# A hybrid attention and DeltaNet block on one core: query and key projections with two terms in one instruction, inverses by alternate columns, transfers and output banks on other queues and pools

## The chip, the core and the metric

The kernel runs on one core of a Trainium2 chip. The core has a matrix engine (PE, whose weight loads the profile lists as PEld), a vector engine (DVE), a scalar engine (ACT), a general engine (POOL) and a queue engine (SP) that here only issues transfers. ACT and POOL can issue transfers too. Each engine works through its own list of instructions in order and waits for the others by semaphores. The metric is the device time of the program in microseconds (us), the median of several runs.

## What is computed

One decoder layer over 256 positions of 1024 channels, all in float32. The input `x` is normalised to `h`; one projection gives twelve parts. Two branches follow: causal softmax attention of 8 heads (suffix `a`), and a gated delta rule of 8 heads in chunks of 64 (suffix `b`). Both are gated, projected, merged and projected again.

```python
h = rmsnorm(x, pre_norm_w)
proj = jnp.einsum('bsd,de->bse', h, w_in)              # 1024 -> 10256
(q_a, k_a, v_a, z_a, q_b, k_b, v_b, z_b, beta_logit, decay_logit, gate_a, gate_b) = jnp.split(proj, IN_OFFSETS, axis=-1)
o_a = moba_attention(partial_rope(heads(q_a), pos), partial_rope(heads(k_a), pos), heads(v_a))
y_a = (o_a * silu(z_a)) @ w_branch_a
q_b, k_b, v_b = split(silu(causal_dwconv(concat(q_b, k_b, v_b), conv_w)))
o_b = gated_deltanet(q_b, k_b, v_b, g, beta)           # solves (I + M) sol = rhs, M strictly lower
y_b = (rmsnorm(o_b, gdn_norm_w) * silu(z_b)) @ w_branch_b
merged = sigmoid(gate_a) * y_a + sigmoid(gate_b) * y_b
return x + rmsnorm(merged @ w_out, post_norm_w)
```

## The kernel before

**Numbers.** A plain float32 product takes several passes of PE. The large projections are therefore made of three products in the one-pass type `float32r`: each operand is split into a high part and the rest, and `hi*Hh + hi*Hl + lo*Hh` are summed in one bank of PSUM. `hi` and `lo` belong to a weight tile, `Hh` and `Hl` to the transposed normalised input (`Xh`, `Xl` to the input without its row factor).

**Slots.** The weights come in 104 slots, in a fixed order (`add`, `pair`, `piece`): v of `a` (slots 0 to 7); then four groups of six slots with two each of k of `b`, q of `b`, q of `a` (8 to 31); four groups of two v of `b` and two k of `a` (32 to 47); the z's (48 to 63), the gates (64 to 79), the branch projections `wa`, `wb` (80 to 95) and the output projection `wo` (96 to 103). For each slot SP loads `raw` (`load`, five buffers in turn), ACT copies it to `hi`, and DVE makes `lo` from both (`prep`). A load is issued when the `lo` of five slots before is made. `projT` makes 128 channels by 256 positions with 24 matmuls of 256 columns; `projN` makes 12 matmuls of 512 columns.

**The planner.** The work around the projections is written as Python generators: `conv` (three steps `acc` on DVE), `unit` (per head k·k and q·k, tile `kk`, then `Mall` and `AV`), `factors`, `inverses`, `vnat`, `head` (the delta rule, tile `dl`), `ybtask`, `ropetask`, `att`, `merge`. While PE's list is written, `tick()` lets each generator go on whose input is ready by a table of costs (`cost_v`, `cost_a`, `dma`, `at`). So each engine's order is fixed when the program is built. DVE and ACT run what the planner put in their lists, in that order, even when a later instruction could already start.

**Banks.** PSUM has three banks for projections (`psP`, taken by `palloc`, given back by `pfree`) and five for the other work (`psM`, taken by `take` or `mbank`, given back by `give`).

**Inverses.** After `factors` has scaled `Mall`, `inverses` (L772) inverts the 64 diagonal 32x32 blocks by substitution, all at once on 128 partitions. Four ACT transfers write the blocks to DRAM (`dN`), two read them back transposed (`Nt`); 31 steps j follow, two DVE instructions each on `m` columns by `31 - j` rows (tile `NtTt`). Each partition has 16 columns of its block, the even partitions 0 to 15 and the odd ones 16 to 31, so `m = min(j + 1, 16)` columns are not zero at step j. Then ACT writes the result to DRAM (`dT`) and reads it back in four transfers (`DT`), for which `head` waits.

**Decays.** `betadecay` (L590) loads 16 rows of decays (`Grow`), subtracts in four DVE instructions of 512 elements in a row, and ACT takes absolute value and exponential in eight.

**Rope.** `ropetask` turns q and k of `a` in six DVE instructions (tile `rt`) after transfers on POOL, and writes them back through DRAM on POOL (`dq2`, then `qa`, `ka`), for which `att` waits.

**The end.** `merge` transposes the merged rows into a `psM` bank (tile `mT`), from which ACT and DVE make `mH`, `mL`; slots `wo` use four more `psM` banks (`po`).

Of the kernel before, what the change touches and what calls it, by code (L numbers as in the profile page):

```python
# [9 lines left out]
F32 = mybir.dt.float32  # L10
# [27 lines left out]
def tile_moba_gdn_block(  # L38
# [108 lines left out]
        q.dma_start(dst, src)  # L147

    cst = ctx.enter_context(tc.tile_pool(name="cst", bufs=1))
    big = ctx.enter_context(tc.tile_pool(name="big", bufs=11))  # L150
    dp = ctx.enter_context(tc.tile_pool(name="dp", bufs=16))
    wp = ctx.enter_context(tc.tile_pool(name="wp", bufs=4))
    tmp = ctx.enter_context(tc.tile_pool(name="tmp", bufs=2))
# [5 lines left out]
    def bigt(name, dt=F32):  # L159
        return big.tile([P, 2048], dt, tag="big", name=name)  # L160
# [245 lines left out]
        return ps  # L406


    def projN(i, pss, lh, ll, kk):
        wh, wl = wts.pop(i)  # L410
        order = [(j, t, m) for j in range(2) for t in range(NT) for m in range(3)]
        if kk == 3 or i == 4:
            order.sort(key=lambda e: e[1])
        if i < 3:
            order.sort(key=lambda e: (e[2] == 2, e[1]))
        for n, (j, t, m) in enumerate(order):
            k = 2 * kk + j
# [65 lines left out]
    gdnw = parT[:, 96:97]  # L483
    Xh = bigt("Xh", F32R).rearrange("p (k s) -> p k s", k=KT)
    Xl = bigt("Xl", F32R).rearrange("p (k s) -> p k s", k=KT)
    Hh = bigt("Hh", F32R).rearrange("p (k s) -> p k s", k=KT)
    Hl = bigt("Hl", F32R).rearrange("p (k s) -> p k s", k=KT)
    xh, xl = (lambda k: Xh[:, k, :]), (lambda k: Xl[:, k, :])
    hh, hl = (lambda k: Hh[:, k, :]), (lambda k: Hl[:, k, :])

# [29 lines left out]
    for _ in xrows(0):  # L520
        pass
    at(clk["T"])
    warmup(8)
    at(0.0)
    prepnow(0, True)

# [63 lines left out]
    def betadecay():  # L590
# [69 lines left out]
        for q in range(4):  # L660
            us = slice(4 * q, 4 * q + 4)
            V.tensor_tensor(Grow[:, us, :], Grow[:, us, :], sm[:, GN, us].unsqueeze(2).to_broadcast([P, 4, P]),
                            op=OP.subtract)
        yield
        act(sm[:, EGL, :], sm[:, EGL, :], AF.Exp)
        for q in range(4):
            us = slice(4 * q, 4 * q + 4)
# [104 lines left out]
    def inverses():  # L772
        yield from need("fac0", "fac1")

        dN = dr.tile([4, 16, 32, 32], F32, name="dN")
        NT_ = bigt("NtTt")
        Nt = NT_[:, 0:1024].rearrange("p (i j) -> p i j", i=32)
        Tt = NT_[:, 1024:1536].rearrange("p (c i) -> p c i", c=16)
        op = NT_[:, 1536:2048].rearrange("p (c i) -> p c i", c=16)
        DT[0] = bigt("DT").rearrange("p (u s) -> p u s", u=16)  # L780
        yield
        for b in range(4):
            dma(nc.scalar, dN[b].rearrange("u i j -> i u j"), Mall[32 * b:32 * b + 32, :, 32 * b:32 * b + 32])
        t0 = cur[0]
        dma(nc.gpsimd, Tt.rearrange("p c i -> p (c i)"), c_rope[:, 512:1024])
        G.memset(DT[0], 0.0)
        at(t0)
        yield
        for hf in range(2):
            dma(nc.scalar, Nt[hf:P:2].rearrange("p i j -> p (i j)"), dN.rearrange("b u i j -> (b u) (i j)"))  # L790
        yield
        for b in range(4):
            t0 = cur[0]
            G.memset(Mall[32 * b:32 * b + 32, :, 32 * b:32 * b + 32], 0.0)
            at(t0)
        for j in range(31):
            n = 31 - j

            m = min(j + 1, 16)
            V.tensor_tensor(op[:, :m, :n], Tt[:, :m, j:j + 1].to_broadcast([P, m, n]),  # L800
                            Nt[:, j + 1:32, j].unsqueeze(1).to_broadcast([P, m, n]), op=OP.mult)
            V.tensor_tensor(Tt[:, :m, j + 1:32], Tt[:, :m, j + 1:32], op[:, :m, :n], op=OP.subtract)
            if j % 2 == 1:

                at(cur[0] - 2.0)
                yield
        dT = dr.tile([4, 16, 32, 32], F32, name="dT")
        yield
        dma(nc.scalar, dT.rearrange("b u c i -> (b u c i)").rearrange("(p n) -> p n", p=P), Tt.rearrange("p c i -> p (c i)"))
        yield  # L810
        for b in range(4):
            dma(nc.scalar, DT[0][32 * b:32 * b + 32, :, 32 * b:32 * b + 32], dT[b].rearrange("u c i -> c u i"))
        at(cur[0] + 5.0)
        done("dt")

    def vnat(h, v2):
# [282 lines left out]
    for i, (kind, n, src, c0) in enumerate(slots):  # L1099
# [20 lines left out]
        elif kind in ("qa", "ka"):  # L1120
            dst = qa if kind == "qa" else ka
            if n == 0:
                dst[0] = bigt(kind).rearrange("p (k s) -> p k s", k=KT)
            ps = projT(i, hh, hl, f"p{kind}{n}")
            act(dst[0][:, n, :], ps, AF.Copy)
            pfree(pids[0] - 1)
            done(f"{kind}{n}")
        elif kind == "va":
# [30 lines left out]
        elif kind in ("wa", "wb"):  # L1159
# [6 lines left out]
            if kk == 0:  # L1166
                grp[kind] = [palloc(f"p{kind}{c}{t}") for t in range(NT)]
                if kind == "wa" and c == 0:
                    mH = bigt("mH", F32R).rearrange("p (k s) -> p k s", k=KT)
                    mL = bigt("mL", F32R).rearrange("p (k s) -> p k s", k=KT)  # L1170
                    xr = bigt("xr").rearrange("p (t d) -> p t d", t=NT)
                    pwt = bigt("pwt")[:, 0:D]
                    ob = bigt("ob").rearrange("p (t d) -> p t d", t=NT)
# [18 lines left out]
        elif kind == "wo":  # L1192
# [3 lines left out]
                grp["wo"] = {}  # L1196
                act(warm[:, 129:130], tw, AF.Sqrt)
            if kk == 0:
                grp["wo"][c] = [mbank(f"po{t}{c}") for t in range(NT)]
            for t in range(NT):  # L1200
                drain(f"mg{kk // 2}{t}")
                at(max(cur[0], flags[f"mg{kk // 2}{t}"]))
# [25 lines left out]
def _constants():  # L1228
# [9 lines left out]
    tt = np.zeros((P, 16, 32), np.float32)  # L1238
    for p in range(P):
        for c in range(16):  # L1240
            tt[p, c, 16 * (p % 2) + c] = 1.0
    rope[:, 512:1024] = tt.reshape(P, 512)
    return {"c_sq": sq, "c_rope": rope}

# [24 lines left out]
```

## Time and profile before

| | us |
|---|---|
| median of 3 runs | 381.87 |
| lowest and highest run | 380.86, 381.88 |
| the profiled execution, its own time | 381.31 |
| its span in the trace | 379.6 |
| PE busy | 365.5 (96%) |
| DVE busy | 279.5 (74%) |
| ACT busy | 202.5 (53%) |
| POOL busy | 29.9 (8%) |

The span begins at the first instruction and ends at the last; 1.7 us of the profiled execution's time lie outside it. A matmul's row covers its way through the engine, and the next one begins before it has ended. So the cost of one in a row of them is the distance from start to start, and a busy share of 96% does not say that PE loses only 4%. A wait for several things is put down to the one that came last.

### The profile page before, as it was taken

Reading aid. Unit: us, or ns where it says so; the run is one execution under the profiler, and the core shown is the slowest. Engines: PE = TensorE matmul, PEld = TensorE weight load, DVE = VectorE, ACT = ScalarE, POOL = GpSimd, SP = SyncE. Lnnn points to the kernel's source line nnn. Section 1 sums busy time; section 2 is a strip of 40 time slices with the busy share of each in tenths; the row PEclk is TensorE's granted clock in tenths of the full one; section 3 lists DMA queues with packets and bytes.
Section 4 is the critical chain, followed back from the end, with each engine's and each line's share of the span. In section 5 each row is a group of like instructions: output and inputs, shape, how many; then the busy total and the mean of one; then the engine's idle time right before and its main releaser. Section 6 shows DMA issues by size and latency. Waiting matters only on the chain.

```text
span 379.6 us, 6307 instructions
## 1 busy us (share of the span) xinstructions
PE 365.5 (96%) x2300; PEld 326.2 (86%) x2300; DVE 279.5 (74%) x639; ACT 202.5 (53%) x405; POOL 29.9 (8%) x53
## 2 busy tenths in 40 slices
PE   8999999999999999989979999999999999999992
PEld 8777999999999999978868799989988888888681
DVE  3987895989987875999995364775898756666544
ACT  3758579455465546645433575456466753344431
POOL 2300000230200321011021000000100000000000
PEclk9999999999999999999999999999999999999998
DMA  7995954865767497469459943234634356656002
GB/s 232 354 255 141 244 145 108 221 168 130 205 167 182 135 237 226 129 180 265 144 179 287 260 142 108 59 108 112 212 107 139 103 165 208 181 172 202 14 0 111
DMA packets 70193, 63.92 MB, mean 168 GB/s; under 512 B 7793, under 2 KB 52194, under 8 KB 70162
## 3 DMA queue, kind: packets, MB, share of 16 engines
q1 hardware_dynamic: 61584, 56.50, 51.6%
q0 software_dynamic: 1680, 4.40, 3.9%
q10 hardware_dynamic: 6898, 2.62, 2.9%
q8 instruction: 18, 0.29, 0.3%
q14 instruction: 13, 0.11, 0.1%
HBM read 60.88 MB, written 2.63 MB: 167 GB/s over the span
## 4 chain that ended last, share of the span: by engine, by line
PE 72%; DVE 14%; DMA 5%; ACT 4%; issue 2%; ACTq 0%; DVEq 0%; POOL 0%; POOLq 0%
PE dl L129 7%; PE pva L129 6%; PE pgb L129 6%; PE pwa L129 6%; PE pga L129 6%; PE pwb L129 6%; PE po L129 6%; DVE lo L117 5%; PE pqb L129 5%; PE pqa L129 5%; DVE NtTt L117 5%; PE pkb L129 4%; PE pvb L129 3%; PE s L129 3%; DMA raw<-in_w_in_dram 3%
## 5 line engine op out<-in xcount | busy, mean ns | idle before, releaser
L117 DVE TENSOR_TENSOR lo<-raw,hi 128x1024 fp32r<-128x1024 f32 (+1 forms) x105 | 126.9, 1216 | 34.8 <-ACT hi L117 33.7
L117 ACT ACTIVATE hi<-raw 128x1024 fp32r<-128x1024 f32 x101 | 106.4, 1055 | 60.0 <-PE pza L129 13.3
L117 DVE TENSOR_TENSOR NtTt<-NtTt 128x112 f32<-128x112 f32 (+27 forms) x62 | 23.7, 382 | 3.0 <-DMA NtTt<-dN 1.3
L129 PE MATMUL pwa<-hi,ya 128*128 128x512 f32 x64 | 20.8, 399 | 0.0
L129 PE MATMUL pwb<-hi,yb 128*128 128x512 f32 x64 | 19.7, 389 | 0.0
L129 PE MATMUL pka<-Hh,hi 128*128 128x256 f32 x64 | 18.3, 287 | 0.7 <-DVE accv L117 0.7
L129 PE MATMUL pvb<-Hh,hi 128*128 128x256 f32 x64 | 18.9, 295 | 0.0
L129 PE MATMUL pkb<-Hh,hi 128*128 128x256 f32 x64 | 18.8, 293 | 0.0
L129 PE MATMUL pkb<-Hl,hi 128*128 128x256 f32 x64 | 18.2, 285 | 0.5 <-DVE Hl L117 0.5
L129 PE MATMUL pqb<-Hh,hi 128*128 128x256 f32 x64 | 18.6, 291 | 0.0
L129 PE MATMUL pqa<-Hh,hi 128*128 128x256 f32 x64 | 18.6, 290 | 0.0
L129 PE MATMUL pqb<-Hh,lo 128*128 128x256 f32 x64 | 18.2, 284 | 0.2 <-DVE lo L117 0.2
L129 PE MATMUL pqa<-Hh,lo 128*128 128x256 f32 x64 | 18.1, 283 | 0.0
L129 PE MATMUL pkb<-Hh,lo 128*128 128x256 f32 x64 | 18.1, 283 | 0.0
L129 PE MATMUL pqa<-Hl,hi 128*128 128x256 f32 x64 | 18.1, 283 | 0.0
L129 PE MATMUL pqb<-Hl,hi 128*128 128x256 f32 x64 | 18.1, 283 | 0.0
L129 PE MATMUL pka<-Hl,hi 128*128 128x256 f32 x64 | 18.1, 283 | 0.0
L129 PE MATMUL pka<-Hh,lo 128*128 128x256 f32 x64 | 18.1, 283 | 0.0
L129 PE MATMUL pvb<-Hh,lo 128*128 128x256 f32 x64 | 18.1, 283 | 0.0
L129 PE MATMUL pvb<-Hl,hi 128*128 128x256 f32 x64 | 18.1, 283 | 0.0
L117 DVE SCALAR_TENSOR_TENSOR acck<-pkb,parT,acck 128x255 f32<-128x255 f32 (+2 forms) x24 | 11.6, 481 | 7.9 <-ACT acck L117 7.3
L129 PE MATMUL pga<-hi,Hh 128*128 128x512 f32 x32 | 14.5, 453 | 0.3 <-ACT za L117 0.3
(383 smaller groups left out, 1041.5 us busy)
## 6 DMA issues: line engine op xcount, KB each, us to landing
raw<-in_w_in_dram SPq DMA_DIRECT2D x79, 512.0 KB, 4.4
raw<-in_w_branch_a_dram SPq DMA_DIRECT2D x8, 512.0 KB, 4.1
raw<-in_w_branch_b_dram SPq DMA_DIRECT2D x8, 512.0 KB, 4.1
raw<-in_w_out_dram SPq DMA_DIRECT2D x8, 512.0 KB, 4.3
x<-in_x_dram SPq DMA_DIRECT2D x4, 256.0 KB, 6.2
Grow<-dg ACTq DMA_DIRECT2D x2, 512.0 KB, 6.3
xr<-in_x_dram POOLq DMA_DIRECT2D x2, 512.0 KB, 3.9
out_dram<-ob SPq DMA_DIRECT2D x2, 320.0 KB, 2.2
```

The costliest lines, as they stand in the source:

```text
L117: LOG(self.e, c, fn(out, *a, **k))
L129: LOG("T", 0, nc.tensor.matmul(out, l, r, **k))
```

## The change

- `projH` takes the place of `projT` for q and k of `a` (16 slots). `Hh` and `Hl` now lie in one tile `H2`, so that `hi*Hh` and `hi*Hl` are one matmul of 512 columns into the two halves of a bank; `lo*Hh` stays one of 256 columns. ACT copies the second half, DVE adds the first one to it, and the bank is given back only then. 128 matmuls fewer are issued: 2088 before, 1956 after, with four warm-up matmuls that are dropped too.
- The warm-up after the first transposes is 4 matmuls, not 8.
- `betadecay` goes back to the planner after each of its four subtractions.
- In `inverses` the columns alternate between a pair of partitions, so that `m = j // 2 + 1`. The sum over the 31 steps of columns by rows is 2856, not 4776. `dN`, `Nt` and `DT` are issued by POOL and SP in turn, `DT` in eight pieces, not four. `dT` stays on ACT. The planner reckons `DT` to be there 16 us after `dT`, where it took 5 us after the last issue.
- `mH` and `mL` lie where `Hh` and `Hl` were, and the pool of large tiles has 9 buffers, not 11.
- The two `po` banks of the second half of the output come from `psP`, not from `psM`.

```diff
+    def projH(i, name):
+        hi, lo = wts.pop(i)
+        ps = palloc(name)
+        for k in range(KT):
+            for m in ((0, 1) if k == 0 else (1, 0)):
+                if m == 0:
+                    T.matmul(ps, hi[:, k, :], H2[:, :, k, :], start=(k == 0), stop=(k == KT - 1))
+                else:
+                    T.matmul(ps[:, 0:S], lo[:, k, :], Hh[:, k, :], start=False, stop=False)
+            if k < KT - 1:
+                tick()
+        return ps
...
+    H2 = cst.tile([P, 2, KT, S], F32R, name="H2")
+    Hh, Hl = H2[:, 0], H2[:, 1]
...
-    warmup(8)
+    warmup(4)
...
-        yield
+            yield 1.4
...
-            dma(nc.scalar, dN[b].rearrange("u i j -> i u j"), Mall[32 * b:32 * b + 32, :, 32 * b:32 * b + 32])
+            dma((nc.gpsimd, nc.sync)[b % 2], dN[b].rearrange("u i j -> i u j"), Mall[32 * b:32 * b + 32, :, 32 * b:32 * b + 32])
...
-            dma(nc.scalar, Nt[hf:P:2].rearrange("p i j -> p (i j)"), dN.rearrange("b u i j -> (b u) (i j)"))
+            dma((nc.gpsimd, nc.sync)[hf], Nt[hf:P:2].rearrange("p i j -> p (i j)"), dN.rearrange("b u i j -> (b u) (i j)"))
...
-            m = min(j + 1, 16)
+            m = j // 2 + 1
...
         for b in range(4):
-            dma(nc.scalar, DT[0][32 * b:32 * b + 32, :, 32 * b:32 * b + 32], dT[b].rearrange("u c i -> c u i"))
-        at(cur[0] + 5.0)
+            for e in range(2):
+                dma((nc.gpsimd, nc.sync)[e], DT[0][32 * b + e:32 * b + 32:2, :, 32 * b:32 * b + 32],
+                    dT[b, :, e].rearrange("u c i -> c u i"))
+        at(t0 + 16.0)
...
-            ps = projT(i, hh, hl, f"p{kind}{n}")
-            act(dst[0][:, n, :], ps, AF.Copy)
+            ps = projH(i, f"p{kind}{n}")
+            act(dst[0][:, n, :], ps[:, S:2 * S], AF.Copy)
+            V.tensor_tensor(dst[0][:, n, :], ps[:, 0:S], dst[0][:, n, :], op=OP.add)
...
-                    mH = bigt("mH", F32R).rearrange("p (k s) -> p k s", k=KT)
-                    mL = bigt("mL", F32R).rearrange("p (k s) -> p k s", k=KT)
+                    mH, mL = Hh, Hl
...
-                grp["wo"][c] = [mbank(f"po{t}{c}") for t in range(NT)]
+                grp["wo"][c] = [(palloc if c else mbank)(f"po{t}{c}") for t in range(NT)]
```

The planner then sets other orders. In the rows below, the number behind a tile's name is its slot or head, and the one behind the underscore is a buffer. First DVE's list around slots 21 to 23, before:

```order
L117 TENSOR_TENSOR lo21_905<-raw21_775,hi21_904 128x1024
L117 SCALAR_TENSOR_TENSOR Mall_175,sm_164<-kk2_930,sq_81 128x128 x2
L117 TENSOR_TENSOR Mall_175<-kk2_930,Grow_165 128x2x128
L117 TENSOR_TENSOR AV2_952<-kk2_930,Grow_165 128x256
L117 TENSOR_TENSOR lo22_944<-raw22_862,hi22_943 128x1024
L117 TENSOR_TENSOR lo23_986<-raw23_869,hi23_985 128x1024
L117 SCALAR_TENSOR_TENSOR acck4_1018<-pkb4_988,parT_125,acck4_1018 128x255
```

and now, from the second `qa` addition on:

```order
L117 TENSOR_TENSOR qa_650<-pqa3_911,qa_650 128x256
L117 SCALAR_TENSOR_TENSOR acck4_969<-pkb4_940,parT_125,acck4_969 128x255
L117 SCALAR_TENSOR_TENSOR acck4_969<-pkb4_940,parT_125,acck4_969 128x254
L117 SCALAR_TENSOR_TENSOR acck4_969<-pkb4_940,parT_125,acck4_969 128x253
L117 TENSOR_TENSOR lo22_909<-raw22_810,hi22_908 128x1024
L117 SCALAR_TENSOR_TENSOR acck5_1010<-pkb5_977,parT_125,acck5_1010 128x255
L117 SCALAR_TENSOR_TENSOR acck5_1010<-pkb5_977,parT_125,acck5_1010 128x254
L117 SCALAR_TENSOR_TENSOR acck5_1010<-pkb5_977,parT_125,acck5_1010 128x253
L117 SCALAR_TENSOR_TENSOR Mall_170,sm_159<-kk2_1002,sq_81 128x128 x2
L117 TENSOR_TENSOR Mall_170<-kk2_1002,Grow_160 128x2x128
L117 TENSOR_TENSOR AV2_1024<-kk2_1002,Grow_160 128x256
L117 TENSOR_TENSOR lo23_938<-raw23_821,hi23_937 128x1024
```

The `lo` of slots 22 and 23, which stood ahead of `acck4` (made of slot 20's result), now stand behind it, that of slot 23 behind `acck5` (of slot 21's) too.

Second, the end of DVE's inverse and the rope (tile `rt`), before:

```order
L117 TENSOR_TENSOR lo57_2322<-raw57_2249,hi57_2321 128x1024
L117 TENSOR_TENSOR rt_2178<-rt_2178,rope_2174 128x512 x2
L117 TENSOR_TENSOR rt_2178<-rt_2178 128x512
...
L117 TENSOR_TENSOR NtTt_1760<-NtTt_1760 128x16x3 x2
L117 TENSOR_TENSOR NtTt_1760<-NtTt_1760 128x16x2 x2
L117 TENSOR_TENSOR lo58_2344<-raw58_2277,hi58_2343 128x1024
L117 TENSOR_TENSOR lo59_2374<-raw59_2298,hi59_2373 128x1024
L117 TENSOR_TENSOR NtTt_1760<-NtTt_1760 128x16 x2
```

and now:

```order
L117 TENSOR_TENSOR lo58_2225<-raw58_2158,hi58_2224 128x1024
L117 TENSOR_TENSOR NtTt_1772<-NtTt_1772 128x15x3 x2
L117 TENSOR_TENSOR NtTt_1772<-NtTt_1772 128x15x2 x2
L117 TENSOR_TENSOR rt_2082<-rt_2082,rope_2078 128x512 x2
L117 TENSOR_TENSOR rt_2082<-rt_2082 128x512
...
L117 TENSOR_TENSOR NtTt_1772<-NtTt_1772 128x16 x2
L117 TENSOR_TENSOR lo59_2253<-raw59_2175,hi59_2252 128x1024
```

The rope stands one slot later, between the `lo` of slots 58 and 59, and the last step of the inverse now stands ahead of `lo59`, not behind it. (Each list has two groups of three `rt` instructions; one is shown.)

Third, PE's list in the output projection, `po` with its column half as the second digit, before:

```order
L129 MATMUL po00_3856<-hi96_3795,mH_3501 128x512
L133 MATMUL mT10_3862<-sq_81,mwb1_3849 128x128 x4
L129 MATMUL po00_3856<-hi96_3795,mL_3502 128x512
L129 MATMUL po00_3856<-lo96_3796,mH_3501 128x512
L129 MATMUL po10_3857<-hi96_3795,mH_3501 128x512
...
L133 MATMUL mT11_3868<-sq_81,mwb1_3849 128x128 x4
L129 MATMUL po01_3884<-hi97_3813,mH_3501 128x512
```

and now:

```order
L129 MATMUL po00_3743<-hi96_3682,H2_128 128x512
L133 MATMUL mT10_3749<-sq_81,mwb1_3736 128x128 x4
L129 MATMUL po00_3743<-hi96_3682,H2_128 128x512
L129 MATMUL po00_3743<-lo96_3683,H2_128 128x512
L129 MATMUL po10_3744<-hi96_3682,H2_128 128x512 x2
L129 MATMUL po10_3744<-lo96_3683,H2_128 128x512
L129 MATMUL po01_3771<-hi97_3700,H2_128 128x512 x2
L129 MATMUL po01_3771<-lo97_3701,H2_128 128x512
L129 MATMUL po11_3772<-hi97_3700,H2_128 128x512
L133 MATMUL mT11_3755<-sq_81,mwb1_3736 128x128 x4
```

The transposes `mT10` and `mT11` stay near their places; `po01`, which stood behind both and had to wait for their bank, now has one of its own and stands ahead of `mT11`.

On the other queues: ACT's list loses `dN`, `Nt` and `DT`; SP's has two `dN` and one `Nt` between the loads of slots 46 and 47, and four `DT` between those of slots 67 and 68; POOL's has its four `DT` ahead of the two rope transfers `qa` and `ka`. The first `dl` matmuls of PE stand behind slot 65, before behind slot 64.

## Rows read from the trace of the kernel before

**Rows 1.** The page: busy time of the engines, and the granted clock in fortieths of the span
```profile
PE 365.5 (96%) x2300; PEld 326.2 (86%) x2300; DVE 279.5 (74%) x639; ACT 202.5 (53%) x405; POOL 29.9 (8%) x53
...
PEclk9999999999999999999999999999999999999998
```

**Rows 2.** PE's waits: who waited for whom, us in all, times, longest
```profile
PE pza L129 <- DVE lo L117: 2.2, 1, 2.2
...
PE po L129 <- DVE mL L117: 0.8, 1, 0.8
PE pka L129 <- DVE accv L117: 0.7, 1, 0.7
...
PE pzb L129 <- DVE accv L117: 0.5, 1, 0.5
PE vT L133 <- ACT v L117: 0.4, 1, 0.4
PE pga L129 <- ACT za L117: 0.3, 1, 0.3
...
PE pqb L129 <- DVE lo L117: 0.2, 1, 0.2
```

**Rows 3.** Timeline of PE: start, duration; nine matmuls of 256 columns, then of 512
```profile
59.75 0.28 PE L129 MATMUL pkb<-Hh,hi 128*128 128x256 f32 x1
...
60.84 0.28 PE L129 MATMUL pqb<-Hh,hi 128*128 128x256 f32 x1
...
200.55 0.39 PE L129 MATMUL pza<-hi,Hh 128*128 128x512 f32 x1
...
202.59 0.39 PE L129 MATMUL pza<-hi,Hh 128*128 128x512 f32 x1
```

**Rows 4.** Busy time by engine in two stretches, us of the span
```profile
90.00:100.00 10.00, 10.00 (x81) 9.84 (x80) 9.45 (x26) 5.38 (x11) 0.76 (x2) 1.00 0.59 151
...
148.00:200.00 52.00, 48.64 (x284) 42.31 (x284) 49.24 (x94) 25.90 (x40) 5.55 (x10) 1.00 0.60 174
```

**Rows 5.** Timeline of DVE: an operation of 256 PSUM elements, inverse steps, rope
```profile
68.96 0.41 DVE L117 TENSOR_TENSOR AV<-kk,Grow 128x256 f32<-128x256 f32 x1
...
172.48 2.25 DVE L117 TENSOR_TENSOR NtTt<-NtTt 128x255 f32<-128x255 f32 x4
...
191.94 1.29 DVE L117 TENSOR_TENSOR rt<-rt,rope 128x512 f32<-128x512 f32 x2
...
196.04 0.90 DVE L117 TENSOR_TENSOR NtTt<-NtTt 128x48 f32<-128x48 f32 x4
```

**Rows 6.** The page's costliest groups: the inverse steps on DVE
```profile
L117 DVE TENSOR_TENSOR NtTt<-NtTt 128x112 f32<-128x112 f32 (+27 forms) x62 | 23.7, 382 | 3.0 <-DMA NtTt<-dN 1.3
```

**Rows 7.** Timeline of ACT and its queue, with the idle time before and its releaser
```profile
141.88 1.15 ACTq L147 DMA_DIRECT2D NtTt<-dN  x2
143.09 0.38 ACT L117 ACTIVATE ka<-pka 128x256 f32<-128x256 f32 x1 [2.90 <-issue]
...
199.58 0.35 ACTq L147 DMA_DIRECT2D dT<-NtTt  x1
...
207.38 4.29 ACTq L147 DMA_DIRECT2D DT<-dT  x4
...
211.77 2.96 ACT L117 ACTIVATE hi<-raw 128x1024 fp32r<-128x1024 f32 x3 [6.47 <-PE pza L129]
```

**Rows 8.** Timeline of PE around the first head
```profile
217.24 0.39 PE L129 MATMUL pga<-lo,Hh 128*128 128x512 f32 x1
217.72 0.68 PE L129 MATMUL dl<-DT,Mall 128*128 128x128 f32 x4
```

**Rows 9.** Timeline of the start: warm-up, and the last input rows with their matmul
```profile
5.75 1.95 PE L129 MATMUL wps<-warm 128*128 128x128 f32 x16
...
16.95 1.13 DVE L117 SCALAR_TENSOR_TENSOR Xl<-xT,parT,Xh 128x128 fp32r<-128x128 f32 x4
...
17.41 0.44 PE L129 MATMUL pva<-hi,Xl 128*128 128x512 f32 x1
```

More of the change, by code (lines that the diff above doesn't have):

```diff
@@ L149, in tile_moba_gdn_block @@
     cst = ctx.enter_context(tc.tile_pool(name="cst", bufs=1))
-    big = ctx.enter_context(tc.tile_pool(name="big", bufs=11))
+    big = ctx.enter_context(tc.tile_pool(name="big", bufs=9))
     dp = ctx.enter_context(tc.tile_pool(name="dp", bufs=16))
@@ L485, in tile_moba_gdn_block @@
     Xl = bigt("Xl", F32R).rearrange("p (k s) -> p k s", k=KT)
-    Hh = bigt("Hh", F32R).rearrange("p (k s) -> p k s", k=KT)
-    Hl = bigt("Hl", F32R).rearrange("p (k s) -> p k s", k=KT)
+    H2 = cst.tile([P, 2, KT, S], F32R, name="H2")
+    Hh, Hl = H2[:, 0], H2[:, 1]
     xh, xl = (lambda k: Xh[:, k, :]), (lambda k: Xl[:, k, :])
@@ L806, in inverses @@
                 yield
-        dT = dr.tile([4, 16, 32, 32], F32, name="dT")
+        dT = dr.tile([4, 16, 2, 16, 32], F32, name="dT")
         yield
-        dma(nc.scalar, dT.rearrange("b u c i -> (b u c i)").rearrange("(p n) -> p n", p=P), Tt.rearrange("p c i -> p (c i)"))
+        dma(nc.scalar, dT.rearrange("b u e c i -> (b u e c i)").rearrange("(p n) -> p n", p=P), Tt.rearrange("p c i -> p (c i)"))
         yield
+        t0 = cur[0]
         for b in range(4):
-            dma(nc.scalar, DT[0][32 * b:32 * b + 32, :, 32 * b:32 * b + 32], dT[b].rearrange("u c i -> c u i"))
-        at(cur[0] + 5.0)
+            for e in range(2):
+                dma((nc.gpsimd, nc.sync)[e], DT[0][32 * b + e:32 * b + 32:2, :, 32 * b:32 * b + 32],
+                    dT[b, :, e].rearrange("u c i -> c u i"))
+        at(t0 + 16.0)
         done("dt")
@@ L1240, in _constants @@
         for c in range(16):
-            tt[p, c, 16 * (p % 2) + c] = 1.0
+            tt[p, c, 2 * c + p % 2] = 1.0
     rope[:, 512:1024] = tt.reshape(P, 512)
```

## The prediction, made before the changed kernel ran

> **What bounds the kernel now.** I read four views in this order. The page first: PE is busy 96% of the span, and its granted clock is full, 2.4 GHz, in every fortieth but the last [rows 1]. So PE is the bound, and time can be won in two ways only: less work for PE, or fewer places where it stands still. Then PE's waits [rows 2]: besides two in the first 40 us that the change doesn't touch (not among the rows), seven are left, 5.1 us in all. Then the timeline of PE, for what an instruction costs [rows 3]: nine matmuls of 256 columns take 60.84 - 59.75 = 1.09 us, 0.121 each; nine of 512 take 202.59 - 200.55 = 2.04 us, 0.227 each. A row of 512 lasts 0.39, that is 0.16 more than its distance to the next. A wait is counted from the end of a row, so each costs about 0.16 us more than it shows: the seven cost 5.1 + 7 x 0.16 = 6.2 us. Last, busy time by stretches [rows 4]: in 148 to 200 us, where the inverse steps run, DVE is busy 49.24 of 52 us. There DVE sets the pace, and PE waits for its `lo` and `acc`.
>
> **Part by part.** I make the sum against the profiled execution's own 381.31 us.
>
> *512 columns.* In 16 slots, 8 pairs each, 2 x 0.121 becomes 0.227, the `lo` matmul stays: 128 x 0.015 = 1.9 us less, all on PE. But the two runs of `H2` that one instruction reads lie apart, and no row shows a `float32r` matmul that reads so. The bounds are 1.9 (as the contiguous 512) and 0 (as two of 256, 0.242). I take 1.8, since the number of columns is that of the rows of 512, and keep 0 for the range. The Trainium skill's page "TensorE: Matmul & The Clock Gate", section "Back-to-back issue gap", speaks against this part: it makes the gap N/2.4 ns plus 2.5 ns, so a dropped instruction would save only 2.5 ns and the whole part 0.3 us; the rows, at 0.121 and 0.227, show some 14 ns per instruction beyond the columns, and I go by them.
>
> *Additions on DVE.* Each of these slots now costs DVE one operation on 256 elements from PSUM, 0.41 us by its nearest kin [rows 5]; 16 of them are 6.6 us. Where do they lie? In the slots of k, q of `b` and q of `a`, two per group of six slots (some 17 us): 0.5 us in every 10, where DVE is already busy 9.45 of 10 [rows 4]. So DVE is about full there. And the planner has put `lo` behind more work than before: in the list shown ahead, `lo23` waits for `acck5`, which waits for slot 21 to end, so only slot 22 is left for a copy on ACT, three `acc`, four operations on `kk` and `lo` itself. That's about the length of a slot with a `kk` pair, so PE is held by some tenths. I find about three such places and charge 1.0 us. The bounds are 0 (the `lo` are just in time) and 6.6 (every addition on the path); I take a value near the low end, since DVE has to catch up only the difference between its fill and PE's.
>
> *Decays in turns.* The wait of `pqb` for `lo` stands right behind the burst of `Grow` work: 0.2 + 0.16 = 0.4 us [rows 2]. Now the subtractions are spread and `lo17` and `lo18` stand ahead of `acck3`. Gain 0.4; what is late next is the item above.
>
> *Alternate columns.* Steps of 255 elements take 2.25/4 = 0.56 us, those of 40 on average 0.90/4 = 0.225: 1.57 ns per element [rows 5]. 2 x 1920 elements fewer are 6.0 us of the 23.7 [rows 6]. In the stretch of 52 us DVE then has 49.24 - 6.0 + three additions x 0.41 = 44.5 us of work, while PE's own is 52 less the stalls, about 48. DVE stops being the bound by 3.5 us. The waits of `pza`, `pka` and `pzb`, 2.2 + 0.7 + 0.5 + 3 x 0.16 = 3.9 us, have this cause [rows 2]. The largest follows the rope, which holds DVE from 191.94 to 196.04 [rows 5]. It still does, now ahead of `lo59`: PE is spared only if `lo58` is well ahead by then. I count 3.5 of 3.9 as gained; at worst the rope keeps 2.0 of it.
>
> *Other queues.* ACT works in order: at 141.88 it had waited for `dN` to land before it could issue `Nt`, and `ka` and `v` came late (idle 2.90); before `DT` it waited for `dT`, and `hi` started 6.47 us late [rows 7]. Two waits of PE hang on that, `vT` for `v` and `pga` for `za`: 0.4 + 0.3 + 2 x 0.16 = 1.0 us [rows 2], all gained, since ACT has no transfer left to wait for but `dT`. On SP the loads of slots 47 and 68 and all later ones now queue behind `Nt` and `DT`, thus behind the landing of `dN` and `dT`; they are issued five slots (some 14 us) ahead of use, and `dT` took 207.38 - 199.58 = 7.8 us [rows 7], so that hides; without that cover it would cost a slot's wait of a few us. The Trainium skill's page "DMA: Bandwidth & Descriptors", section "Issuing engines are not separate DMA queues", says that transfers from several engines share the same 16 DMA engines and that more issuers save only issue time, which is usually small. By that the transfers get no shorter, and I count them so; but the rows show that here an issue also holds ACT for its wait, which is what I count as gained.
>
> *Output banks.* `po01` no longer waits for the bank of `mT10`: the wait of `po` for `mL`, 0.8 + 0.16 = 1.0 us, goes [rows 2]. What comes next, `mL` for the second half, is needed two slots later. `mH` and `mL` in the place of `Hh` and `Hl`, and nine large buffers, cost nothing: what lay there was last read by the gates, 16 slots earlier; without that distance `merge` would wait for a slot.
>
> *Warm-up.* Four of eight are 1.95/2 = 1.0 us less ahead of the first projection [rows 9]. But the last input rows `Xl` start at 16.95, and PE used them at 17.41 [rows 9]; the first of the four was ready at 16.95 + 1.13/4 = 17.23. That chain hangs on loads and ACT, not on PE, so no more than 0.2 survives it. I take 0.1, with 0 and 1.0 as bounds.
>
> *Sum:* -1.8 - 0.4 + 1.0 - 3.5 - 1.0 - 1.0 - 0.1 = -6.8 us, **374.5 us**. The median of the runs stands 0.56 above the profiled execution; that lies inside the range.
>
> **Rivals.** *A: two runs cost as two instructions.* Then the first part gives 0: 376.3 us. For it speaks that no row shows such a read, against it that the columns are the same. The Trainium skill's page "TensorE: Matmul & The Clock Gate", section "Back-to-back issue gap", comes close to this rival: with its 0.3 us the sum would be 376.0.
>
> *B: the rope still stops PE.* DVE is held 4.1 us plus the last inverse step, longer than a slot of 12 x 0.227 = 2.7 us; if `lo58` is less than 2 us ahead, PE stands about as long as before: 374.5 + 1.6 = 376.1 us.
>
> *C: the additions fill DVE.* If DVE falls behind by most of the 6.6 us through slots 8 to 47, the part costs 5.5, not 1.0: 379.0 us. For it: 9.45 busy of 10. Against it: DVE's idle time there is made of waits for ACT, which a backlog uses up.
>
> *D: slower, by the inverse's way back.* The first `dl` needs `DT`. Before, PE was through with slot 64 at 217.24 + 0.23 and started `dl` at 217.72 [rows 8], 18.1 us after `dT` was issued [rows 7]: that chain was already just in time. Now `dl` stands a slot later (+2.7) and PE comes there 5.8 us sooner (the sum up to there), at about 214.4; the last inverse step stands ahead of `lo59` and so is through by about 194, and 18.1 later is 212.1. Margin 2 us. But half of `DT` now goes through POOL, behind the rope's transfers, in twice as many pieces. Each us beyond the margin stops PE for one. From 9 us more the gain is gone, at 10 the kernel is slower: a chain of 28 us instead of 18.1, 382.5 us.
>
> **How the numbers follow.** Forecast as summed: 0.57. A: 0.12. B: 0.13. C: 0.10. D with all its price: 0.05. Two or more together, near no change: 0.03. The likeliest gives 374.5. The bounds of the forecast: all of the stalls, the warm-up's 1.0 and no late `lo` would give 372.2; A and B together 378, C 379. The range from 372.2 to 378.5 leaves out D, the mixed cases and the upper half of C. A measurement of this kernel tells about 0.3% (1.1 us) from no change: faster by more than that 0.89 (the forecast, A, B and most of C), within it 0.06, slower 0.05.
>
> **What would show it.** In the trace after: PE's waits without `pza`, `pka`, `pzb` and `vT` of more than 0.3 us; `pqa` matmuls 0.227 and 0.121 apart in turn (A: 0.24); DVE's `NtTt` at about 18 us, and below 95% busy there; ACT without `dN`, `Nt` and `DT` on its queue; `po` without its wait. New waits of `pqb`, `pkb` for `lo` in 60 to 110 us are the charged 1.0, or C; a wait of `dl` for a transfer is D. I'm wrong if PE's list is no longer the bound, or if a wait at one place only moves to the next slot.

## The result and the profile after

The changed kernel takes 377.17 us (median of 4 runs, 376.67 to 377.32) where the kernel before took 381.88 us (380.86 to 382.88, 4 runs). The ratio is 0.9874, with a 95% interval of 0.9847 to 0.9902: 4.7 us less, faster by more than the 0.3% that can be told from no change. The profiled execution of the changed kernel took 376.67 us and has a span of 375.0 us, 4.6 us less than the span before; the sum of the prediction was 6.8 us.

The page of the changed kernel answers to [rows 1] and [rows 6]. PE still sets the end, at a full granted clock, and the inverse steps are 18.1 us of DVE, where they were 23.7:

```profile
PE 364.4 (97%) x2164; PEld 317.0 (85%) x2164; DVE 279.0 (74%) x656; ACT 202.6 (54%) x405; POOL 33.1 (9%) x60
...
PEclk9999999999999999999999999999999999999999
...
L117 DVE TENSOR_TENSOR NtTt<-NtTt 128x126 f32<-128x126 f32 (+22 forms) x62 | 18.1, 292 | 1.6
```

PE's waits, whole this time, answer to [rows 2] (who waited for whom, us in all, times, longest):

```profile
PE wps L129 <- POOL warm L117: 1.1, 1, 1.1
PE pzb L129 <- DVE ka L117: 1.1, 1, 1.1
PE pkb L129 <- DVE H L117: 0.5, 1, 0.5
PE vT L133 <- ACT v L117: 0.5, 1, 0.5
PE psbd L129 <- issue: 0.3, 1, 0.3
PE pka L129 <- DVE lo L117: 0.2, 1, 0.2
```

The waits of `pza`, of `pka` and `pzb` for `accv`, of `po`, `pga` and `pqb` are gone, and no `dl` waits for a transfer. In their place stand a new wait of `pzb` for `ka`, one of `pka` for `lo`, and one of `vT` for `v` that is no shorter than before. (`wps`, `pkb` and `psbd` are in the first 40 us, where the change touches only the warm-up, `wps`. They stand in the list of before too: three waits, where the prediction spoke of two.) Busy time in the longer stretch of [rows 4]; the columns are PE, PEld, DVE, ACT, POOL, then granted clock, DMA share and GB/s:

```profile
148.00:200.00 52.00, 50.91 (x259) 42.52 (x260) 47.52 (x98) 26.57 (x42) 11.53 (x21) 1.00 0.77 231
```

From 148 to 200 us PE now is busy 50.91 of 52 us, 48.64 before: most of the stalls that went lay there. The third view is the timeline of PE (start, duration), which answers to [rows 3]. Six pairs of `pqa`, then 33 matmuls of 256 columns, then 30 of 512, and last two stalls:

```profile
52.07 0.40 PE L129 MATMUL pqa<-H,hi 128*128 128x512 f32 x1
...
54.18 0.39 PE L129 MATMUL pqa<-H,hi 128*128 128x512 f32 x1
...
73.99 0.40 PE L129 MATMUL pkb<-H,hi 128*128 128x256 f32 x2
...
77.89 0.28 PE L129 MATMUL pkb<-H,hi 128*128 128x256 f32 x1
...
147.16 0.40 PE L129 MATMUL pka<-H,hi 128*128 128x512 f32 x1
148.03 0.44 PE L133 MATMUL vT<-sq,v 128*128 128x128 f32 x2 [0.47 <-ACT v L117]
...
164.74 0.39 PE L129 MATMUL pzb<-lo,H 128*128 128x512 f32 x1
166.19 0.73 PE L129 MATMUL pzb<-hi,H 128*128 128x512 f32 x2 [1.06 <-DVE ka L117]
...
189.62 0.63 PE L129 MATMUL pza<-hi,H 128*128 128x512 f32 x2
...
196.61 0.63 PE L129 MATMUL pza<-hi,H 128*128 128x512 f32 x2
```

A pair costs 2.11/6 = 0.352 us, not the forecast 0.227 + 0.121 = 0.348 and not far below the 3 x 0.120 of before. And two prices have changed that the change doesn't mention. A matmul of 256 columns that streams `H` is 3.90/33 = 0.118 (before 0.121). One of 512 that holds `H` in the array and streams `hi` is 6.99/30 = 0.233 (before 0.227), though nothing in it was edited but the place of `H`.

### The profile page after: what moved, and what is told of

It reads as the page before. It is cut to its first block, busy times and chain, and to the rows that moved or that the text cites. A ratio compares the mean times of both kernels' runs of the same rounds, so it can differ in the third digit from the quotient of the medians.

```text
span 375.0 us, 6054 instructions
## 1 busy us (share of the span) xinstructions
PE 364.4 (97%) x2164; PEld 317.0 (85%) x2164; DVE 279.0 (74%) x656; ACT 202.6 (54%) x405; POOL 33.1 (9%) x60
## 4 chain that ended last, share of the span: by engine, by line
PE 89%; DVE 6%; ACT 2%; DMA 1%; issue 1%; SPq 0%; POOL 0%; DVEq 0%; ACTq 0%
PE dl L129 7%; PE pqb L129 6%; PE pqa L129 6%; PE pva L129 6%; PE po L129 6%; PE pza L129 6%; PE pgb L129 6%; PE pga L129 6%; PE pwa L129 6%; PE pzb L129 6%; PE pwb L129 6%; PE pkb L129 6%; PE pka L129 4%; PE pvb L129 3%; PE s L129 3%; DVE lo L117 2%
## 5 line engine op out<-in xcount | busy, mean ns | idle before, releaser
L129 PE MATMUL pgb<-hi,H 128*128 128x512 f32 x64 | 24.3, 436 | 0.0
L129 PE MATMUL pkb<-H,hi 128*128 128x256 f32 x128 | 23.8, 286 | 0.5 <-DVE H L117 0.5
L129 PE MATMUL pqb<-H,hi 128*128 128x256 f32 x128 | 24.0, 287 | 0.0
L129 PE MATMUL pvb<-H,hi 128*128 128x256 f32 x128 | 23.0, 282 | 0.0
L129 PE MATMUL pka<-H,hi 128*128 128x512 f32 x64 | 23.0, 397 | 0.0
L129 PE MATMUL pqa<-H,hi 128*128 128x512 f32 x64 | 22.7, 396 | 0.0
L129 PE MATMUL pga<-hi,H 128*128 128x512 f32 x64 | 22.7, 426 | 0.0
L129 PE MATMUL pzb<-hi,H 128*128 128x512 f32 x64 | 20.3, 398 | 1.1 <-DVE ka L117 1.1
L129 PEld LDWEIGHTS pkb<-H,hi 128*128 128x128 f32 x128 | 20.1, 188 | 1.0 <-DVE H L117 0.7
L129 PE MATMUL po<-hi,H 128*128 128x512 f32 x64 | 20.6, 398 | 0.0
L129 PE MATMUL pwb<-hi,yb 128*128 128x512 f32 x64 | 19.7, 389 | 0.0
L117 DVE TENSOR_TENSOR NtTt<-NtTt 128x126 f32<-128x126 f32 (+22 forms) x62 | 18.1, 292 | 1.6
```

Source lines behind the costliest of these rows:

```text
L117: LOG(self.e, c, fn(out, *a, **k))
L129: LOG("T", 0, nc.tensor.matmul(out, l, r, **k))
```

## The experiments

The new place was the first suspect. `Hh` and `Hl` were tiles of the pool `big`; they and the weights all began at 32 bytes beyond a multiple of 64, and were alike modulo 2048, by the addresses in the built program. `H2` lies in the pool `cst` and begins at a multiple of 256, 32 bytes off the weights' grid. Three runs move these starts by padding, with the order of the instructions kept; a fourth takes the 512-column instruction back.

**All large tiles at 32 modulo 64.**

```diff
-    H2 = cst.tile([P, 2, KT, S], F32R, name="H2")
+    H2p = cst.tile([P, 4112], F32R, name="H2")
+    H2 = H2p[:, 8:4104].rearrange("p (w k s) -> p w k s", w=2, k=KT)
```

> The changed kernel with 32 bytes more ahead of H2 and 32 behind it, so that H2 starts at 32 modulo 64 bytes as Hh and Hl did before, and every other large tile stays at 32 modulo 64. The order of instructions is the changed kernel's. Theory 1, the start address: in the changed kernel H2 starts at 0 modulo 64 while the weights start at 32, and that is why the 512-column rows with H in them went from 0.227 to 0.234 and the 256-column ones from 0.120 to 0.117. Then here pza, pzb and po go back to 0.227 (384 instructions with the gates, by 0.002 to 0.007: 2.3 us less), pkb, pqb, pvb back to 0.120 (576 by 0.0023: 1.3 us more), and pqa, pka come in pairs of 0.227 + 0.120 = 0.347 in place of 0.351 (128 pairs: 0.5 us less): 375.6 us against 377.2. Theory 2, the place of H2 in the memory or its being one tile: nothing changes, 377.2 us, 0.234 and 0.117 stay. Theory 3 (the first rival of the prediction), two runs cost as two instructions: the pqa instruction of 512 stays at 0.233 to 0.240 whatever the address.

374.99 us, ratio to before 0.9820 (0.9807 to 0.9834), so 2.1 us less than the changed kernel's 0.9874 by ratios, with the same instructions in the same order. Its timeline, 21 matmuls of 512 that stream `hi`, and five pairs of `pqa`:

```profile
52.66 0.40 PE L129 MATMUL pqa<-H,hi 128*128 128x512 f32 x1
...
54.43 0.40 PE L129 MATMUL pqa<-H,hi 128*128 128x512 f32 x1
...
187.78 0.62 PE L129 MATMUL pza<-hi,H 128*128 128x512 f32 x2
...
192.58 0.62 PE L129 MATMUL pza<-hi,H 128*128 128x512 f32 x2
```

The `pza` matmuls went from 0.233 to 4.80/21 = 0.229, the pair of `pqa` stayed at 1.77/5 = 0.354, and the 256-column ones stayed at 0.118 by the starts of all of them. So 32 bytes have a price, against theory 2. Theory 1 had the sign and nearly the size, but not all rows: it wanted 0.227, 0.120 and 0.347. And `pqa`'s 512 columns stayed at 0.235 as theory 3 said.

**All later tiles at 0, and `H2` alone at 32.** In the first the padding stands behind `H2` only (`[P, 4104]`, slice `0:4096`), in the second ahead of it only (slice `8:4104`).

> The changed kernel with 32 bytes more behind H2 only: H2 stays at 0 modulo 64 bytes and all later large tiles, the weights among them, move to 0 modulo 64. Theory 1a, it counts whether the two operands start alike modulo 64: 0.227 and 0.120 everywhere, as with all at 32, 375.6 us. Theory 1b, it counts where each operand starts by itself (streamed at 0: 0.117; weights at 0 under a stream at 32: 0.234): the stream of 512 columns from hi gets faster too, towards 0.223, or stays at 0.234; time 374 to 377. Theory 2, the place: 377.2 us and no row changes.

374.51 us, ratio 0.9813 (0.9794 to 0.9831).

> The changed kernel with 32 bytes more ahead of H2 only: H2 at 32 modulo 64 bytes, the later large tiles at 0. Theory 1a (alike or not): not alike, so 0.234 and 0.117 as in the changed kernel, 377.2 us. Theory 1b (each by itself): 256 columns streamed from H2 at 0.120 or more, 512 streamed from hi at another value than 0.234; time 374 to 379. Theory 2: 377.2 us, no row changes.

376.92 us, ratio 0.9869 (0.9855 to 0.9883). So when `H2` and the weights are alike modulo 64, it is 374.5 to 375.0 us, whichever multiple they are on, and when they are 32 apart, 376.9 to 377.2 us, whichever of them is moved. That speaks for theory 1a against 1b: what counts is how the two starts lie to each other, not either by itself.

**One run of 512.** The layout of `H2` is turned, so that the two parts lie side by side for each k; padding as with all at 32.

```diff
-    H2 = H2p[:, 8:4104].rearrange("p (w k s) -> p w k s", w=2, k=KT)
+    H2 = H2p[:, 8:4104].rearrange("p (k w s) -> p w k s", w=2, k=KT)
```

> The changed kernel with the starts of H2 and the weights alike modulo 64 bytes, and H2 laid out so that the 256 columns of the high and of the low part lie side by side for each k: the instruction of 512 reads one run of 512, not two of 256. The order of instructions is that of the run with all at 32. Theory 3 (the prediction's first rival: two runs cost as two instructions): pqa and pka come down from 0.235, which is 2 x 0.118, to the 0.229 of the other 512-column rows, 128 x 0.006 = 0.8 us less than the 375.0 of that run: 374.2 us. Rival: it isn't the two runs but that H2 is streamed here where it is the held operand elsewhere: 0.235 and 375.0 us stay.

374.98 us, ratio 0.9827 (0.9810 to 0.9845), beside 0.9820 with two runs. Five pairs of its timeline:

```profile
52.55 0.40 PE L129 MATMUL pqa<-H,hi 128*128 128x512 f32 x1
...
54.32 0.40 PE L129 MATMUL pqa<-H,hi 128*128 128x512 f32 x1
```

1.77/5 = 0.354 again. So the price of the 512 columns is no matter of two runs, and theory 3 falls as a mechanism. What is left is a difference: 0.235 where `H` is streamed, 0.229 where `hi` is. That the streaming of `H` makes it, as the rival has it, isn't shown, since these matmuls of 512 columns also alternate with some of 256 and the others don't; no run separates the two. Why it is so stays open.

**Three of 256 again, no additions.**

```diff
-            ps = projH(i, f"p{kind}{n}")
-            act(dst[0][:, n, :], ps[:, S:2 * S], AF.Copy)
-            V.tensor_tensor(dst[0][:, n, :], ps[:, 0:S], dst[0][:, n, :], op=OP.add)
+            ps = projT(i, hh, hl, f"p{kind}{n}")
+            act(dst[0][:, n, :], ps, AF.Copy)
```

> The changed kernel with q and k of a made by three instructions of 256 columns again, and without the additions on DVE; H2, the alternate columns, queues and banks stay. Theory 1: with H2 at 0 modulo 64 bytes three of 256 are 3 x 0.117 = 0.351, and the pair of 512 and 256 is 0.234 + 0.117 = 0.351 as well, so the instruction of 512 brings nothing here, and what goes are the stalls that the additions brought: pzb for ka 1.2 us and some of pka for lo and vT for v (0.3 to 1.0): 375.0 to 376.0 us. The prediction's reckoning (three of 256 dearer by 1.8 us, the additions worth 1.0) would have 378.0 us.

374.58 us, ratio 0.9810 (0.9796 to 0.9824): undoing the first item of the change makes it 2.4 us faster by ratios. (The planner moves other work with it: the first `dl` stands at 205.1 us here, at 216.2 in the changed kernel.) PE's waits, whole, and seven triples of `pqa`:

```profile
PE wps L129 <- POOL warm L117: 1.1, 1, 1.1
PE pqa L129 <- DVE lo L117: 0.6, 1, 0.6
PE pkb L129 <- DVE H L117: 0.6, 1, 0.6
PE psbd L129 <- issue: 0.3, 1, 0.3
...
51.82 0.40 PE L129 MATMUL pqa<-H,hi 128*128 128x256 f32 x2
...
54.31 0.40 PE L129 MATMUL pqa<-H,hi 128*128 128x256 f32 x2
```

A triple costs 2.49/7 = 0.356, the pair 0.352. Over all such matmuls of the trace (the means of their distances added up, pauses and switches of type left out), it is 0.3551 against 0.3515: 128 x 0.0036 = 0.5 us is all that the instruction of 512 brings here. The waits of `pzb` for `ka`, of `pka` for `lo` and of `vT` for `v` are gone, and one new wait has come. Where did the additions hurt? DVE's list in the changed kernel (start, duration), with ACT's copy of `ka6` ahead:

```profile
161.44 0.38 ACT L117 ACTIVATE ka<-pka 128x256 f32<-128x256 f32 x1 [1.09 <-PE pka L129]
...
161.86 1.51 DVE L117 SCALAR_TENSOR_TENSOR accv<-pvb,parT,accv 128x255 f32<-128x255 f32 x3
163.29 1.38 DVE L117 TENSOR_TENSOR NtTt<-NtTt 128x115 f32<-128x115 f32 x4
164.59 1.22 DVE L117 TENSOR_TENSOR lo<-raw,hi 128x1024 fp32r<-128x1024 f32 x1
165.72 0.75 DVE L117 TENSOR_TENSOR ka<-pka,ka 128x256 f32<-128x256 f32 x2
```

ACT is done with `ka6` at 161.8. The addition stands behind three other jobs of DVE and starts at 165.72, and only it gives the bank back. With the banks of `ka6` and `ka7` not given back and one taken by the first half of `zb`, none of the three `psP` banks is free, and the second half of `zb` waits 1.06 us.

**Start addresses without the additions.** Three of 256, with the padding of all at 32; the weights then lie 64 bytes off `H2` modulo 256. And once more with a distance of 128 (96 bytes behind `H2`, none ahead).

> Three instructions of 256 columns for q and k of a, no additions on DVE (as in the run with three of 256), and 32 bytes more ahead of H2 and behind it, so that H2 and the weights start alike modulo 64 bytes (they differ by 64 modulo 256). Theory 1a (start addresses alike or not): the 512-column rows of the z's, gates and po go from 0.233 to 0.229 (480 by 0.0042: 2.0 us less), the 256-column ones stay at 0.118 (960 by 0.0005: 0.5 us less): 374.6 - 2.5 = 372.1 us. If the address's gain hangs on the additions or the 512 columns of q and k, 374.6 us stays.

370.61 us, ratio 0.9718 (0.9699 to 0.9737): the fastest of all, 2.8% below before and 6 us below the changed kernel. Its timeline: 21 matmuls of 256, 39 more of them at another place, 21 of 512:

```profile
51.76 0.40 PE L129 MATMUL pqa<-H,hi 128*128 128x256 f32 x2
...
54.23 0.40 PE L129 MATMUL pqa<-H,hi 128*128 128x256 f32 x2
...
83.92 0.39 PE L129 MATMUL pqb<-H,hi 128*128 128x256 f32 x2
...
88.34 0.39 PE L129 MATMUL pqb<-H,hi 128*128 128x256 f32 x2
...
173.83 0.62 PE L129 MATMUL pzb<-hi,H 128*128 128x512 f32 x2
...
178.64 0.62 PE L129 MATMUL pzb<-hi,H 128*128 128x512 f32 x2
```

0.229 for 512 as expected. The 256-column ones cost 2.47/21 = 0.118 at 52 us and 4.42/39 = 0.113 at 84 us, with the same operands: there are two rhythms. In the starts of the trace one holds until something comes between (a stall, or `kk`, `psq` or `vT`), and which one follows can differ. On average `pka` and `pvb` have 0.1145 here, which no expectation had, and with it the run is 1.5 us faster than expected.

> The same with 96 bytes more behind H2 and none ahead, so that H2 starts at 0 and the weights at 128 modulo 256 bytes. If only the start modulo 64 bytes counts, it is the run with a difference of 64 again: 0.229, 0.118, 372.1 us. If a wider distance counts (before, with all large tiles alike modulo 2048, the rows were 0.227 and 0.120), the rows move towards these: 480 x 0.002 less and 960 x 0.002 more, 373.0 us.

375.03 us, ratio 0.9829 (0.9810 to 0.9849), as slow as with a distance of 32. 21 of its 512-column matmuls:

```profile
174.61 0.62 PE L129 MATMUL pzb<-hi,H 128*128 128x512 f32 x2
...
179.49 0.62 PE L129 MATMUL pzb<-hi,H 128*128 128x512 f32 x2
```

4.88/21 = 0.232, and 0.119 for those of 256. Here the starts are alike modulo 64 as well, so "alike modulo 64" is not the rule; theory 1a falls in this form. What stands is a table by the distance of the starts modulo 256: 0 (before): 0.227 and 0.120; 32: 0.233 and 0.118; 64: 0.229 and 0.114 to 0.118; 128: 0.232 and 0.119. The entry for 0 comes from another kernel, but each of these runs has a check of it: in `pwb` both operands, `yb` and the weights, keep a distance of 0 whatever the padding, and `pwb` stays at 0.227 in all of them, while the rows with `H` move. What makes it stays open.

**Sixteen columns again** (`m = min(j + 1, 16)` with the layout before; the transfers stay on POOL and SP).

> The changed kernel with the columns of the inverses laid out as before (even partitions 0 to 15, odd ones 16 to 31, min(j + 1, 16) columns in step j); the transfers stay on POOL and SP. The prediction's reckoning: DVE gets 5.6 us more work in 145 to 200 us, and PE's waits there, 3.5 of 3.9 us, come back: 380.7 us. Rival, the rope alone: only the wait of pza behind the rope comes back, 2.0 us: 379.2 us. Rival, that the columns bring nothing, since what held PE was the order: 377.2 us.

383.42 us, ratio 1.0054 (1.0029 to 1.0078): 6.9 us slower than the changed kernel by ratios. Rows of PE's waits that the changed kernel doesn't have:

```profile
PE pza L129 <- DVE lo L117: 2.9, 1, 2.9
...
PE s L133 <- ACT p L117: 0.7, 2, 0.6
PE s L133 <- DVE ya L117: 0.7, 1, 0.7
```

The first is the wait behind the rope of [rows 2], longer. The other two are new and lie at 308 to 314 us: with the inverse later, the attention starts later (its first matmul at 229.2 us, in the changed kernel at 219.3), and its last heads come too late for the `wa` slots. By the distances from start to start, `pza` takes 3.2 us more than in the changed kernel, `pwa` and the attention's `s` together 2.7, of the 6.1 by which the span is longer. So the columns are worth more in the changed kernel than the 3.9 us of waits.

**The columns alone, in the kernel before** (transfers on ACT, `DT` in eight pieces).

> The kernel before with the alternate columns alone; transfers stay on ACT, DT in eight pieces. The prediction's reckoning: 3.5 us less: 378.0 us. From the run with sixteen columns, in which undoing them cost 6.2 us: 375.3 us. Rival (the rope, the prediction's second): pza still waits behind the rope, 2.0 us of the 3.9 stay: 379.6 us.

384.56 us, ratio 1.0054 (1.0033 to 1.0075): slower than before. The wait that did it, and the timeline of PE around it:

```profile
PE dl L129 <- DMA DT<-dT: 6.0, 1, 6.0
...
197.68 0.39 PE L129 MATMUL pza<-lo,Hh 128*128 128x512 f32 x1
204.04 1.19 PE L129 MATMUL dl<-DT,Mall 128*128 128x128 f32 x4 [5.98 <-DMA DT<-dT]
...
PEclk9999999999999999999996999999999999999998
```

The waits of `pza`, `pka` and `pzb` are gone here, 3.9 us, all that the prediction counted for this part. But the planner, which still reckons `DT` to be there 5 us after its issue, put `dl` at 197.9, and PE stood 6.0 us for the transfers. This is the wait of the prediction's rival D, though by another way: `DT` is on ACT here, not on POOL behind the rope. Most of it is the place of `dl`, 13.5 us behind the issue of `dT` at 184.36; some may be the eight pieces on ACT, since from `dT` to `dl` it took 19.7 us, before 18.1 [rows 8]. And the stall cost more than its length: in this run the granted clock is 0.50 (1.2 of 2.4 GHz) from 203 to 209 us (the 6 in the row of the page), in the last microsecond of the stall and for five after it. Four matmuls `dl<-DT,Mall` take 1.06 us at 205.67 there, 0.60 in the changed kernel at 216.22, and all distances behind `dl` matmuls add up to 28.4 us, before to 25.6. In the changed kernel, where the planner has the line `at(t0 + 16.0)`, `dl` stands at 216.22 and waits for nothing: the last traced landing of `DT` is at 212.85.

**The transfers on ACT again** (`dN`, `Nt`, `DT` on `nc.scalar`, the rest as changed).

> The changed kernel with dN, Nt and DT issued by ACT again. The prediction's reckoning: ACT is held by its waits for dN and dT, vT waits longer for v and pga for za, 1.0 us: 378.2 us. Rival: in the changed kernel vT still waits 0.5 us for v and no pga waits, so the queues moved little of it: 377.2 to 377.5 us. A second rival: with eight DT transfers queued on ACT after the landing of dT, hi is held longer than before: 379 us or more.

387.59 us, ratio 1.0128 (1.0095 to 1.0160): 9.7 us slower than the changed kernel by ratios. PE's waits that grew, and ACT's list:

```profile
PE pza L129 <- ACT za L117: 4.3, 1, 4.3
PE vT L133 <- ACT v L117: 2.5, 1, 2.5
PE pzb L129 <- DVE ka L117: 1.6, 1, 1.6
...
198.56 7.95 ACTq L147 DMA_DIRECT2D DT<-dT  x8
206.61 2.00 ACT L117 ACTIVATE hi<-raw 128x1024 fp32r<-128x1024 f32 x2 [9.97 <-issue]
...
PEclk9999999999999998999998999999999999999998
```

The second rival of this run holds: eight issues of `DT` keep ACT from `hi` and `za` for 9.97 us. But not all of the 9.7 us is waiting. After the stalls of `vT` and `pza` the granted clock is 0.50 from 152 to 155 and from 210 to 213 us (the two eights in the row of the page), and there matmuls of 512 columns stand 0.43 us apart, not 0.23. No run has four pieces on ACT with the alternate columns, so how much the number of pieces costs isn't shown.

**The po banks from psM again** (`mbank` for all four).

> The changed kernel with all four po banks from psM again. The prediction's reckoning: po01 waits for the bank of mT10 until DVE has read it for mL, 1.0 us: 378.2 us. Rival: the wait was made of the order before (both transposes ahead of po01 and a full psM), which the other changes have altered: 377.2 us.

378.47 us, ratio 0.9904 (0.9884 to 0.9925): 0.0030 x 381.9 = 1.1 us slower than the changed kernel by ratios, but the two intervals overlap (0.9847 to 0.9902 there), so the time doesn't show it. The wait is back:

```profile
PE po L129 <- DVE H L117: 0.8, 1, 0.8
```

**The decays at once**, on the fastest version, with 64 bytes distance (one `yield` behind the four subtractions).

> The run with three of 256 and a difference of 64 bytes, with the four Grow subtractions in a row again. The prediction's reckoning: the wait of 0.4 us behind the burst comes back: 370.6 + 0.4 = 371.0 us. Rival: there pqa waits 0.9 us for lo at 71 us, behind two accumulations and two kk groups that were put late by ACT's seven exponentials of Grow; if taking turns is what bunches these up, the run is faster, 369.7 to 370.6 us.

371.79 us, where before took 382.4 beside it (381.5 beside the version of this run without the edit): ratio 0.9724 (0.9702 to 0.9747), where that version has 0.9718 (0.9699 to 0.9737). No difference can be told. Its trace has the old wait back, where the other had 0.8 us of `pqa` for `lo`:

```profile
PE pqb L129 <- DVE lo L117: 0.4, 1, 0.4
```

So the item takes one wait away and makes another, in this order of the work; the inconclusive time is what both make together.

## Why the prediction was right, and where its sum was not

The time, 377.17 us, lies in the range of 372.2 to 378.5, and the sign is right. The likeliest value, 374.5, was 2.7 too low. The nearest of its cases was rival A with 376.3. The steps that took waits away were right; two other steps were too favourable by 1.3 and 1.5 us, and that the time still lies inside the range is in part luck, as the sum below shows. By its own steps:

- **What bounds the kernel:** right. PE's list is the bound before and after, and the time moved by what PE does and where it stands.
- **Alternate columns (-3.5):** right in mechanism and nearly in size. `NtTt` is at 18.1 us, forecast at about 18. All three waits are gone, here and with the columns alone: 3.9 us. The doubt about the rope (rival B) didn't come true: DVE's rope runs from 189.29 to 193.41 and `lo58` was ready 5.7 us ahead of its use, `lo59` 2.1 us (by the ends of `lo` and the first matmuls that use them), since the inverse was nearly through by then. DVE in 148 to 200 us is busy 47.52 us, not the 44.5 worked out. The sign that the prediction named, below 95%, tells nothing: before it was 49.24 of 52, 94.7%.
- **Other queues (-1.0):** right in kind, half in place. `pga` no longer waits for `za`. `vT` still waits for `v`, now 0.47 us, with no transfer ahead of `v` on ACT any more, only `hi` and two `AV` operations; the wait has changed its cause. That the queues matter much more in the changed kernel, with its eight pieces (9.7 us), was not foreseen. ACT stood 9.97 us in that run, most of it in the 7.95 us of the eight issues. The Trainium skill's page "DMA: Bandwidth & Descriptors", section "Issuing engines are not separate DMA queues", calls the time to issue usually small beside the transfer itself; in this run it isn't small (7.95 us, where the first of these transfers lands 6.7 us after its issue begins), and the engine that issues is the one on which PE waits.
- **Output banks (-1.0):** right as to the wait, which is gone and comes back (0.8 us) with the old banks; as a gain in time it isn't told from noise.
- **Decays (-0.4):** the wait is gone as said; as a gain in time it isn't shown.
- **Warm-up (-0.1):** as far as the trace shows: 0.9 us fewer of `wps`, and 0.8 us more of `pva` behind it.
- **512 columns (-1.8): this step failed.** It took 14 ns of every distance between matmuls for a price per instruction, which goes when the instruction goes. The pair costs 0.3515 where three of 256 at the same addresses cost 0.3551: 0.5 us in all. Rival A was nearer with its price (0), but not with its reason: one run instead of two changes nothing. The Trainium skill, page "TensorE: Matmul & The Clock Gate", section "Back-to-back issue gap", gives 2.5 ns beyond the columns for an isolated matmul, not for a stream of them as here, a limit that the prediction left out; the 0.3 us worked out from it come near the 0.5 of these two runs. With a distance of 64 bytes they don't agree: there the pair has 0.351 (all at 32) and the triple 0.346 on average (the fastest version), so the longer instruction costs 128 x 0.005 = 0.6 us more.
- **Additions (+1.0): mis-sized, and at the wrong places.** `pqb` and `pkb` never wait for `lo` from 60 to 110 us; `lo23` came 0.2 us ahead of its use. What the additions brought are the stalls of `pka` at 120 us (0.35), `vT` at 122 and 148 (0.28 and 0.65) and `pzb` at 165 (1.2), by the distances from start to start beyond the usual: 2.5 us, and all of it is gone without them. The prediction looked at DVE's fill and the `lo`, but not at the bank that the addition now holds, on which the largest of these stalls hangs: a bank freed by ACT's copy of 0.4 us is now freed by DVE after whatever stands ahead, for `ka6` some 4 us later.
- **Not in the sum: the start addresses.** "`mH` and `mL` in the place of `Hh` and `Hl`, and nine large buffers, cost nothing" didn't ask where `H2` begins. By the starts of all matmuls, pauses and switches of type left out: those of 512 with `H` held (480) cost 2.1 us more than before, those of 256 outside of q and k of `a` (576) 0.8 less, those of q and k of `a`, taken as triples at these addresses, 0.6 less. That is 0.7 us more than before, but 2.1 to 2.3 us by ratios more than with a better distance, and 3.5 without the additions.
- **Rival D:** not in the changed kernel. From the issue of `dT` at 193.85 to the last traced landing of `DT` at 212.85 it took 19.0 us, a us more than the 18.1 that the prediction took over from before, and `dl` stood 3.4 us behind it, where the prediction had a margin of 2. The columns alone show such a wait (6.0 us) with the old due time. Whether the due time of 16 us is what keeps it away in the changed kernel isn't shown, since no run changes it alone; the prediction didn't name it.

Summed with what was measured: columns -3.9, queues -1.0 (with `vT`'s old wait), banks -1.0, decays -0.4, warm-up -0.1, 512 columns -0.5, additions +2.5, addresses +0.7 (2.1 - 0.8 - 0.6), and 0.4 for a new stall of `dl` at 233 us: -3.3 us. The span moved by -4.6; 1.3 us are left over, 0.4 of them behind the last matmul. The rest lies at changes between float32 and `float32r`, where the distances behind the 480 and 576 matmuls named above add up to some 1.4 us less than before; why is open. So the terms of the sum were off by 1.3 (512 columns) and 1.5 (additions), both to the same side, and what no term had (addresses, the stall of `dl`, the changes of type) nearly cancels: that part is luck.

## What to carry to other kernels

When a result's bank is given back by another engine than before, read that engine's list at this place and ask when it gets there: its average fill doesn't tell. A stall removed by making one job shorter can come back where a planner trusts a fixed delay for the transfers behind it, as with the columns alone, so look at the due time with the work. And after moving a tile, compare the distance between matmuls that read it, before blaming or crediting the edit; padding of 32 bytes was worth 2.1 to 2.3 us here, as much as most of the edits.

## What the hardware showed unexpectedly

The distance from one `float32r` matmul to the next changed with the distance between the start addresses of its two operands: 0.229 to 0.233 us for 512 columns and 0.114 to 0.119 for 256, with no other edit than padding (0.227 and 0.120 in the kernel before). For one and the same pair of operands there are two steady rhythms, 0.113 and 0.118, and an interruption can change from one to the other. A matmul that streams 512 columns of `H` and alternates with one of 256 cost 0.235 beside others of 512 at 0.229, whether the columns lay side by side or in two parts; in this kernel an instruction of 512 is about as dear as two of 256. The granted clock was full in all these stretches, so it isn't the clock. It was not full everywhere: with the columns alone and with the transfers on ACT it was 0.50 for 3 to 6 us, after PE had stood still for 2.5, 4.3 and 5 us, so a stall there cost more than the profile's wait says.
